# Modulation rows in two or three buffers in turn, narrow loads in their own buffers, and work put off by a tile, in a float32 decoder block

## The chip, the cores and the metric

The kernel runs on one core of one Trainium2 chip. Its metric is the device time of one execution in microseconds (us). The engines of a core work side by side, each on its own queue in program order: TensorE (PE) for matrix products, VectorE (DVE), ScalarE (ACT), GpSimd (POOL), and SyncE (SP), which here issues the transfers.

## The reference

One decoder block on 512 tokens of 1024 features, all in float32. A modulation vector of nine parts shifts, scales and gates three sub-layers: a SwiGLU, a token mixer and a second SwiGLU. A final norm ends it.

```python
mod = silu(c) @ w_ada + b_ada              # 9 x 1024
sh1, sc1, gt1, sh2, sc2, gt2, sh3, sc3, gt3 = split(mod, 9)
h = h + 0.5 * gt1 * swiglu(rmsnorm(h) * (1 + sc1) + sh1)
u = rmsnorm(h) * (1 + sc2) + sh2
p, q, k, v, gate_logits = split(u @ w_in)
y_pool = (trailing means over 2, 4, 8, 16 tokens, minus the token) @ w_pool * pool_scale
q, k = rope(q), rope(k)                    # 12 heads of 64, in 3 groups
y_attn = softmax-weighted sum over groups of dilated window attention(q, k, v)
g_pool, g_attn = split(sigmoid(gate_logits))
h = h + gt2 * ((g_pool * (y_pool @ w_pool_branch) + g_attn * (y_attn @ w_attn_branch)) @ w_out)
h = h + 0.5 * gt3 * swiglu(rmsnorm(h) * (1 + sc3) + sh3)
```

The windows and dilations of the three head groups are (128, 1), (512, 4) and (2048, 16).

## The kernel before, in words

Features lie on the 128 partitions, tokens along the free dimension, so an activation is 8 tiles of 128x512. Each float32 product is made of three matmuls (`mm3`, L353): weight and activation are both split into a high part (rounded) and a low part (the rest), and high x high, high x low and low x high are added in a bank of PSUM.

**Weights.** They come as 128x1024 loads (and some of 128x512) in the order in which they are used. `fetch` (L231) issues the next loads on SyncE's queue as far as buffers are free: three `raw` tiles, and one more during the merge. `split_hi` (L287) makes the high part on ScalarE (L312), `split_lo` (L318) the low part on VectorE (L324), into a ring of 7296 columns. `look` (L333) does this for three or four tiles ahead of the one that TensorE takes next. For products done with fewer multiplications (a Strassen-like scheme on 2x2 blocks: seven products in place of eight) `make` (L250) forms differences of weights on VectorE (L256).

**Modulation rows.** Each of the 72 pieces of `mod` is the sum over a 128x1024 row tile of `w_ada` times `silu(c)`. `ada_fetch` (L370) issues the transfer of a row on SyncE (L374), `ada_do` (L377) makes product and sum on VectorE (L382), and `bg` (L401) is one step of this in the background: it fetches as far as `ada_depth` rows ahead and free buffers allow, makes one product, gives the buffer back and fetches again. The rows 48 to 71 are made in the mixer. From L1271 on they have one buffer, `AR`; after L1343 also `cs`, which held the cosines and sines until then.

**The mixer's attention stage** (`mix`, L1240). Queries and keys of the first head group and its v come first. The loop at L1321 makes the q and k of the groups 1 and 2, in eight tiles of 24 matmuls (`mm_tile`, L1056). Functions hung at a step k of the eight run ahead of that step's matmuls (`hooks`, L1308): at step 5 a piece of attention (scores, maxima and exponentials, a transpose, the product with v), at step 6 the second half of the rotation (`rope_b`, L1050) of the tile before, at step 7 `bg`. Behind a tile's matmuls stands `rope_a` (L1038): ScalarE writes the signed tile to a scratch (L1042), SyncE copies it with the 32-row halves exchanged, in four transfers (L1045), and VectorE multiplies by the cosines (L1047). `rope_b` multiplies the exchanged copy by the sines (L1053) and adds it (L1054). Two tiles with the pooled part follow, whose means GpSimd makes (`pool_diff`, L1199), and then four class tiles with the v of groups 1 and 2: token class c of four, ended by a copy into `v23` (L1375). `v23` is idle between the first rotations, which use it as scratch (L1277), and the second pooling tile.

**The merge** (`merge_out`, L1430). The outputs m = 6, 7, 0, ... 5 are made in pairs. For the last three pairs `gate_duo` (L1393) makes the gate logits in seven products, with ScalarE copying from bank to bank between them (L1396): product 0 goes into bank A, is copied to C, products 2, 4 and 6 are added to A. Then `branch` (L1447), for each of the pair, makes y_pool and y_attn times their branch weights; VectorE multiplies them by the gates and adds them (L1455 to L1457), ScalarE makes the high part (L1458), VectorE the low part (L1459). The high and low parts are read by the output projection only (L1490 to L1505), for whose first two outputs the seven parts other than m = 5 are used first. The gates of the first pair come as plain tiles, whose four sigmoids stand at L1462, ahead of the first branch.

The order of the work on each engine is that of the program text; waits are put in where data or buffers ask for them.

Of the kernel before, what the change touches and what calls it, by code (L numbers as in the profile page):

```python
# [146 lines left out]
class Kernel:  # L147
# [6 lines left out]
    def plan(self):  # L154
# [69 lines left out]
        self.ready = True  # L224
        self.pos, self.held, self.retired, self.half = 0, None, [], None
        self.at, self.start, self.top = {}, {}, 0
        self.buf = {}
# [3 lines left out]
    def fetch(self, n=None):  # L231

        n = len(self.order) - 1 if n is None else min(n, len(self.order) - 1)
        while self.fetched <= self.order[n][1] and self.free:
            i = self.fetched
            name, off, w = self.loads[i]
            src = self.a[name][off:off + P * w].rearrange("(p n) -> p n", p=P)
            self.buf[i] = self.free.pop(0)
            for c in self.pieces(i, w):
                self.nc.sync.dma_start(self.buf[i][:, c], src[:, c])  # L240
            self.fetched += 1
# [76 lines left out]
    def split_lo(self):  # L318
# [9 lines left out]
        for n in [n for n in self.buf if self.last[n] == i]:  # L328
            b = self.buf.pop(n)
            if not any(b is x for x in self.retired):  # L330
                self.free.append(b)

# [44 lines left out]
    def ada_do(self, j, n=1, between=None):  # L377
        t, mod = self.adat.pop(j), self.mod[:, j:j + 1]
        for i in range(n):
# [6 lines left out]
            elif between:  # L386
                between()
        if self.ada_free is not None:
            self.ada_free.append(t)
# [850 lines left out]
    def mix(self):  # L1240
# [10 lines left out]
        with tc.tile_pool(name="rt", bufs=1) as self.rt, tc.tile_pool(name="aw", bufs=2) as self.aw, \  # L1251
# [18 lines left out]
            self.head(1, bk, AF.Exp)  # L1270
            self.ada_free, self.ada_stop, self.ada_depth = [self.AR], 65, 2  # L1271
            self.bg_fetch()
# [14 lines left out]
            for n in range(4):  # L1287
# [11 lines left out]
                for i in ((), (0, 1), (2,), (3,))[n]:  # L1299
                    self.rope_b(*to[i], 1, sw[i])  # L1300
            self.held = None

# [36 lines left out]

            b = self.mm_tile(hooks([], rest + [(6, lambda: by_class(0)), (7, self.bg)]))  # L1340
            self.pool_diff(0, b)

            self.ada_free.append(self.cs)  # L1343
            self.bg_fetch()
            b = self.mm_tile(hooks(g23[0], [(2, lambda: by_class(1)), (3, self.bg), (7, self.bg)]))
# [14 lines left out]
            for c in range(4):  # L1360
                mid = [lambda c=c: by_class(c + 1)] if c in (1, 2) else []
                hk = hooks(g23[c + 1], [(2, self.bg), (7, self.bg)], mid) if c < 3 else \
                    hooks([], [(2, self.at_swap), (2, nxt), (3, nxt), (6, nxt), (7, nxt)])
# [12 lines left out]
            self.held = None  # L1376
            assert self.ada_next == 65 and not self.adat, self.ada_next
            gates = [self.mm_tile(hooks([], [(1, nxt), (3, nxt), (5, self.at_merge)]))]
# [13 lines left out]

    def gate_duo(self, s, c, p5, last):  # L1393

# [10 lines left out]
        for i, (bank, u, start) in enumerate(((A, lambda: blk(lo4, T1), True), (B, lambda: S(0), True),  # L1405
# [3 lines left out]
            if i == 6:  # L1409
                v.tensor_tensor(q(c, 1), q(c, 1), r(p5), op=OP.add)  # L1410
            self.look(4)
            self.product(bank, u(), start, not i)
            if i == 0:
# [3 lines left out]
            elif i == 1:  # L1417
                copy(p5, B)
            elif i == 2:
                copy(q(c, 0), r(A))  # L1420
# [9 lines left out]
    def merge_out(self, ready, last, ma):  # L1430
        nc, tc = self.nc, self.tc
        v = nc.vector
        with tc.tile_pool(name="mg", bufs=1) as mg:
            sc = [mg.tile([P, 2 * T], F32, name=x) for x in ("gs", "gc")]
            p5, raw = mg.tile([P, T], F32, name="p5"), mg.tile([P, D], F32, name="raw")
            self.free.append(raw)
            self.X, self.retired = [self.AR, self.cs], []
            self.ready = True
# [8 lines left out]
            def branch(m):  # L1447
                gp, ga = (x[:, m % 2 * T:(m % 2 + 1) * T] for x in sc)
                self.look()
                w = self.take()  # L1450
                pb, ab = self.nb(), self.nb()
                for b, xh, xl, o in ((pb, self.PH, self.PL, 0), (ab, self.YH, self.YL, 2)):
                    for k in range(2):
                        self.mm3(b, *w[o + k], xh[k], xl[k], k == 0, k == 1)
                v.tensor_tensor(gp, gp, pb, op=OP.mult)  # L1455
                v.tensor_tensor(ga, ga, ab, op=OP.mult)
                v.tensor_tensor(gp, gp, ga, op=OP.add)  # L1457
                nc.scalar.activation(MH[m], gp, AF.Copy)  # L1458
                v.tensor_tensor(ML[m], gp, MH[m], op=OP.subtract)  # L1459

            for i, b in enumerate(ready):
                nc.scalar.activation(sc[i % 2][:, i // 2 * T:(i // 2 + 1) * T], b, AF.Sigmoid)  # L1462
# [26 lines left out]

            kl = [ks(0), ks(1)]  # L1490
            bs = [self.nb(), self.nb()]
# [4 lines left out]
            for m in range(5):  # L1496
# [6 lines left out]
                self.bg()  # L1503
                if m < 2:
                    self.bg()  # L1505
# [7 lines left out]
    def build(self):  # L1513
# [38 lines left out]

        self.ada_free, self.ada_depth = None, 3
        with self.open_ffn():
# [188 lines left out]
```

## Time and profile before

| | |
|---|---|
| median of 3 runs | 1020.76 us (1019.96 to 1021.65) |
| the profiled execution | 1021.9 us |
| its span, first to last instruction | 1020.1 us |
| granted TensorE clock, mean over the span | 0.990 |
| TensorE matmuls busy | 993.1 us (97%) |
| VectorE busy | 788.6 us (77%) |
| ScalarE busy | 475.6 us (47%) |
| GpSimd busy | 30.2 us (3%) |
| read from memory | 135.29 MB |

The attention stage runs from 390.8 to 542.3 us of the span, the merge from there to about 627, the output projection to about 667. A row of a timeline has the start, the duration, the engine, the line, the operation, the tile written and those read, their shapes, the count, and in brackets the idle time ahead of it and what ended it. A row of the waits has who waited, for whom, and the sum in us, the number and the longest. A row of windows has the stretch, its length, then for PE, PEld (weight loads), DVE, ACT and POOL the busy time and the number of instructions, then the granted clock, the share of the transfer engines and GB/s. In the names of tiles `whi` and `wlo` are the high and low parts of weights, `raw`, `AR` and `cs` buffers, `rt` and `tr` scratches of the rotation.

### The profile page before, as it was taken

The page shows a single profiled execution, that of the slowest core. Times are in us where ns is not written, and L with a number is a line of the kernel's source. Part 1 is how long each engine was busy: PE and PEld are TensorE (multiplying, and loading weights), DVE is VectorE, ACT ScalarE, POOL GpSimd, SP SyncE. Part 2 cuts the span into 40 slices and gives each one's busy share as a digit, 9 for nine tenths or more (in the row PEclk, how much of TensorE's full clock was granted, in tenths as well). Part 3 has the DMA queues.
Part 4 walks back from the last instruction along what each step waited for, and adds up shares of the span by engine and source line. Part 5 has one row for each costly group of instructions (what it writes and reads, how often), then busy time and mean ns, then how long its engine had stood idle before and what let it go on. Part 6 is the DMA issues. An engine that isn't in the chain of part 4 may idle for free.

```text
span 1020.1 us, 16353 instructions
## 1 busy us (share of the span) xinstructions
PE 993.1 (97%) x6686; PEld 900.9 (88%) x6686; DVE 788.6 (77%) x1091; ACT 475.6 (47%) x713; POOL 30.2 (3%) x31
## 2 busy tenths in 40 slices
PE   9999999999999999997998999999999999999997
PEld 7888999989899998765778888898899899998997
DVE  7989969898896767767887775877778777776754
ACT  5443643525344554442635453454356345352553
POOL 0000000000000000007200000000000000000002
PEclk9999999999999999998999999999999999999999
DMA  9856445554544425555422225531333325241312
GB/s 341 281 197 220 130 162 182 184 171 165 170 156 135 124 86 150 155 158 182 133 83 76 69 86 185 192 98 62 124 125 126 102 83 166 74 136 53 107 47 83
DMA packets 44876, 141.74 MB, mean 139 GB/s; under 512 B 6273, under 2 KB 9089, under 8 KB 44802
## 3 DMA queue, kind: packets, MB, share of 16 engines
q1 hardware_dynamic: 44226, 140.18, 42.4%
q8 instruction: 52, 0.85, 0.3%
q10 hardware_dynamic: 576, 0.52, 0.2%
q14 instruction: 22, 0.18, 0.1%
HBM read 135.29 MB, written 2.24 MB: 135 GB/s over the span
## 4 chain that ended last, share of the span: by engine, by line
PE 85%; DVE 6%; ACT 3%; DMA 2%; issue 2%; SPq 1%; POOL 0%; POOLq 0%; DVEq 0%; ACTq 0%
PE bank L355 13%; PE bank L356 13%; PE bank L357 13%; PE bank L742 12%; PE bank L743 12%; PE bank L744 12%; PE bank L1669 1%; PE bank L1671 1%; PE bank L1673 1%; DMA rt<-rt 1%; ACT whi L312 1%; DVE AR L382 1%; DVE wlo L324 1%; SPq L1045 1%; DMA rt<-tr 1%
## 5 line engine op out<-in xcount | busy, mean ns | idle before, releaser
L324 DVE TENSOR_TENSOR wlo<-raw,whi 128x1024 fp32r<-128x1024 f32 (+4 forms) x168 | 175.3, 1056 | 54.3 <-ACT whi L312 53.7
L742 PE MATMUL bank<-UH,whi 128*128 128x256 f32 x640 | 177.2, 277 | 0.0
L743 PE MATMUL bank<-UL,whi 128*128 128x256 f32 x640 | 177.2, 277 | 0.0
L744 PE MATMUL bank<-UH,wlo 128*128 128x256 f32 x640 | 177.1, 277 | 0.0
L312 ACT ACTIVATE whi<-raw 128x1024 fp32r<-128x1024 f32 (+4 forms) x168 | 149.9, 910 | 51.7 <-DVE raw L256 47.6
L355 PE MATMUL bank<-HI,whi 128*128 128x512 f32 (+1 forms) x406 | 146.2, 360 | 0.0
L356 PE MATMUL bank<-HK,whi 128*128 128x512 f32 (+1 forms) x406 | 145.9, 359 | 0.0
L357 PE MATMUL bank<-HI,wlo 128*128 128x512 f32 (+1 forms) x406 | 145.8, 359 | 0.0
L324 DVE TENSOR_TENSOR wlo<-X,whi 128x1024 fp32r<-128x1024 f32 (+3 forms) x104 | 111.8, 1083 | 32.4 <-ACT whi L312 32.1
L742 PEld LDWEIGHTS bank<-UH,whi 128*128 128x128 f32 x640 | 120.5, 188 | 0.4
L743 PEld LDWEIGHTS bank<-UL,whi 128*128 128x128 f32 x640 | 120.2, 188 | 0.0
L744 PEld LDWEIGHTS bank<-UH,wlo 128*128 128x128 f32 x640 | 120.1, 188 | 0.0
L742 PE MATMUL bank<-SH,whi 128*128 128x256 f32 x408 | 112.9, 277 | 0.0
L743 PE MATMUL bank<-SL,whi 128*128 128x256 f32 x408 | 112.8, 276 | 0.0
L744 PE MATMUL bank<-SH,wlo 128*128 128x256 f32 x408 | 112.8, 276 | 0.0
L312 ACT ACTIVATE whi<-X 128x1024 fp32r<-128x1024 f32 (+3 forms) x104 | 95.8, 943 | 33.6 <-DVE X L256 32.9
L355 PE MATMUL bank<-UH,whi 128*128 128x512 f32 (+1 forms) x304 | 107.2, 353 | 0.0
L356 PE MATMUL bank<-UL,whi 128*128 128x512 f32 (+1 forms) x304 | 105.8, 348 | 0.1
L357 PE MATMUL bank<-UH,wlo 128*128 128x512 f32 (+1 forms) x304 | 105.6, 347 | 0.0
L357 PEld LDWEIGHTS bank<-HI,wlo 128*128 128x128 f32 x406 | 76.2, 188 | 11.7
L355 PEld LDWEIGHTS bank<-HI,whi 128*128 128x128 f32 x406 | 76.2, 188 | 11.5
L356 PEld LDWEIGHTS bank<-HK,whi 128*128 128x128 f32 x406 | 76.3, 188 | 11.3
(330 smaller groups left out, 1845.0 us busy)
## 6 DMA issues: line engine op xcount, KB each, us to landing
raw<-wmix SPq DMA_DIRECT2D x44, 512.0 KB, 3.8
raw<-wf1i SPq DMA_DIRECT2D x31, 512.0 KB, 4.5
raw<-wf2i SPq DMA_DIRECT2D x30, 512.0 KB, 4.1
AR<-wada SPq DMA_DIRECT2D x25, 512.0 KB, 4.2
ada<-wada SPq DMA_DIRECT2D x23, 512.0 KB, 5.7
cs<-wada SPq DMA_DIRECT2D x16, 512.0 KB, 3.6
X<-wf2i SPq DMA_DIRECT2D x14, 512.0 KB, 3.7
X<-wf1i SPq DMA_DIRECT2D x12, 512.0 KB, 4.4
```

The source lines that it names most:

```text
L312: self.nc.scalar.activation(self.hi[:, y], r[:, x], AF.Copy)
L324: self.nc.vector.tensor_tensor(self.lo[:, y], r[:, x], self.hi[:, y], op=OP.subtract)
L355: M(ps, hi, uh, start=start, stop=False)
L356: M(ps, hi, ul, start=False, stop=False)
L357: M(ps, lo, uh, start=False, stop=stop)
L382: self.nc.vector.scalar_tensor_tensor(t[:, c], t[:, c], 1.0, self.cond[:, c], op0=OP.mult, op1=OP.mult, accum_out=o)
L742: M(o, hi, uh, start=start and p == 0 and k == 0, stop=False, skip_group_check=True)
L743: M(o, hi, ul, start=False, stop=False, skip_group_check=True)
L744: M(o, lo, uh, start=False, stop=k == 3, skip_group_check=True)
L1045: nc.sync.dma_start(w[32 * o:32 * o + 32], t[32 * i:32 * i + 32])
L1669: M(b, hi, self.UH[k], start=k == 0, stop=False)
L1671: M(b, hi, self.UL[k], start=False, stop=False)
```

## The change

1. *Rows.* In the last projection of v of the first group (n = 2) two 4 KB halves of `v23` join `AR` as buffers, and one row product is made there. The loop then has three buffers in turn at depth 2. After the first pooling tile the two halves leave (`ada_gone`: a row in one of them is still used, the buffer is not given back), `cs` joins, and depth is 1. The steps of `bg` move: first pooling tile two in place of one, class tiles one in place of two. Row 64 goes to the output projection, which has three buffers in place of two and eight rows in place of seven.
2. *Narrow loads* of 128x512 (the branch weights) get two buffers of their own in the merge, a piece of `tr` and a new tile.
3. *Work put off.* The four sigmoids, the branches' gate products (`merge`) and the high and low parts (`parts`) go into a list `rest`, of which some are done behind the next `look`: the sigmoids in the first branch, the first branch's products in the second, its parts and the second's products ahead of product 0 of the next `gate_duo`, the second's parts behind product 1; after the last pair between the first splits of the output projection.

```diff
@@ fetch
-        while self.fetched <= self.order[n][1] and self.free:
+        while self.fetched <= self.order[n][1]:
...
+            free = self.small if self.small is not None and w <= T else self.free
+            if not free:
+                break
...
-            self.buf[i] = self.free.pop(0)
+            self.buf[i] = free.pop(0)
@@ split_lo
-                self.free.append(b)
+                (self.small if any(b is x for x in self.smalls) else self.free).append(b)
@@ ada_do
-        if self.ada_free is not None:
+        if self.ada_free is not None and not any(t is x for x in self.ada_gone):
@@ mix
-            self.ada_free, self.ada_stop, self.ada_depth = [self.AR], 65, 2
+            self.ada_free, self.ada_stop, self.ada_depth = [self.AR], 64, 2
...
                 for i in ((), (0, 1), (2,), (3,))[n]:
                     self.rope_b(*to[i], 1, sw[i])
+                if n == 2:
+
+                    mine = [self.v23.rearrange("p n f -> p (n f)")[:, i * D:(i + 1) * D] for i in range(2)]
+                    self.ada_free += mine
+                    self.bg()
...
-            b = self.mm_tile(hooks([], rest + [(6, lambda: by_class(0)), (7, self.bg)]))
+            b = self.mm_tile(hooks([], rest + [(3, self.bg), (6, lambda: by_class(0)), (7, self.bg)]))
             self.pool_diff(0, b)
-            self.ada_free.append(self.cs)
-            self.bg_fetch()
+            self.ada_gone = mine
+            self.ada_free = [x for x in self.ada_free if not any(x is y for y in mine)] + [self.cs]
+            self.ada_depth = 1
...
-                hk = hooks(g23[c + 1], [(2, self.bg), (7, self.bg)], mid) if c < 3 else \
+                hk = hooks(g23[c + 1], [(7, self.bg)], mid) if c < 3 else \
@@ gate_duo
             self.look(4)
+            if not i:
+                rest(2)
             self.product(bank, u(), start, not i)
...
             elif i == 1:
                 copy(p5, B)
+                rest()
@@ merge_out
+            self.small = [self.tr[:, :T], mg.tile([P, T], F32, name="narrow")]
+            self.smalls = list(self.small)
...
                 self.look()
+                if rest:
+                    do()
                 w = self.take()
...
-                v.tensor_tensor(gp, gp, pb, op=OP.mult)
-                v.tensor_tensor(ga, ga, ab, op=OP.mult)
-                v.tensor_tensor(gp, gp, ga, op=OP.add)
-                nc.scalar.activation(MH[m], gp, AF.Copy)
-                v.tensor_tensor(ML[m], gp, MH[m], op=OP.subtract)
-
-            for i, b in enumerate(ready):
-                nc.scalar.activation(sc[i % 2][:, i // 2 * T:(i // 2 + 1) * T], b, AF.Sigmoid)
+                def merge():
+                    v.tensor_tensor(gp, gp, pb, op=OP.mult)
+                    v.tensor_tensor(ga, ga, ab, op=OP.mult)
+                    v.tensor_tensor(gp, gp, ga, op=OP.add)
+
+                def parts():
+                    nc.scalar.activation(MH[m], gp, AF.Copy)
+                    v.tensor_tensor(ML[m], gp, MH[m], op=OP.subtract)
+
+                rest.extend([merge, parts])
+
+            def sigmoids():
+                for i, b in enumerate(ready):
+                    nc.scalar.activation(sc[i % 2][:, i // 2 * T:(i // 2 + 1) * T], b, AF.Sigmoid)
+
+            rest = [sigmoids]
+            do = lambda n=1: [rest.pop(0)() for _ in range(n)]
...
-                    self.gate_duo(*sc, p5, last)
+                    self.gate_duo(*sc, p5, last, do)
...
-            self.ada_free, self.ada_stop = [ma.tile([P, D], F32, name=x) for x in ("k0", "k2")], 72
+            self.ada_free, self.ada_stop, self.ada_depth = [ma.tile([P, D], F32, name=x) for x in ("k0", "k2", "v1")], 72, 2
...
-            kl = [ks(0), ks(1)]
+            kl = [ks(0)]
+            do(2)
+            kl.append(ks(1))
+            do()
...
-                if m < 2:
+                if m < 3:
                     self.bg()
```

More of the change, by code (lines that the diff above doesn't have):

```diff
@@ L225, in plan @@
         self.pos, self.held, self.retired, self.half = 0, None, [], None
+        self.small, self.smalls = None, []
         self.at, self.start, self.top = {}, {}, 0
@@ L1376, in mix @@
             self.held = None
-            assert self.ada_next == 65 and not self.adat, self.ada_next
+            assert self.ada_next == 64 and not self.adat, self.ada_next
             gates = [self.mm_tile(hooks([], [(1, nxt), (3, nxt), (5, self.at_merge)]))]
@@ L1391, in mix, with gate_duo @@
         outer.close()
-    def gate_duo(self, s, c, p5, last):
+    def gate_duo(self, s, c, p5, last, rest):
         nc, v = self.nc, self.nc.vector
@@ L1551, in build @@
         self.scr2 = dram.tile([32, 2 * T], F32, name="scr2")
-        self.ada_free, self.ada_depth = None, 3
+        self.ada_free, self.ada_depth, self.ada_gone = None, 3, []
         with self.open_ffn():
```

## The prediction

> **What bounds the kernel now.** I read the page first, then who waited for whom on TensorE, then stretches of the span with their clock, then the engines' timelines around each wait.
>
> ```profile
> span 1020.1 us, 16353 instructions
> PE 993.1 (97%) x6686; PEld 900.9 (88%) x6686; DVE 788.6 (77%) x1091; ACT 475.6 (47%) x713; POOL 30.2 (3%) x31
> ```
>
> TensorE (PE) is busy for 97% of the span, so a change that leaves the matmuls alone can only win what TensorE waits and what a lowered clock costs it. Its waits of more than 1.1 us in all, by line, are these:
>
> ```profile
> PE bank L742 <- ACT bank L1396: 7.7, 3, 3.5
> PE bank L1091 <- DVE k L1054: 4.5, 1, 4.5
> PE bank L1142 <- DVE v L1375: 3.0, 1, 3.0
> PE bank L1124 <- ACT prob L1112: 2.6, 2, 2.0
> ```
>
> The columns are the sum, the number and the longest. All of them lie in the token mixer: 10.1 us in the attention stage (4.5 + 3.0 + 2.6), 7.7 us in the merge (one wait in each of the three calls of `gate_duo`). The stretches in which the granted clock was halved (column after POOL) lie just behind or in those waits:
>
> ```profile
> 446.40:449.80 3.40, 3.40 (x10) 2.67 (x9) 3.37 (x6) 2.07 (x4) 0.00 (x0) 0.53 0.12 16
> 463.50:470.30 6.80, 4.65 (x13) 3.66 (x14) 5.60 (x5) 0.00 (x0) 6.58 (x5) 0.51 0.20 64
> 487.40:490.80 3.40, 3.40 (x24) 2.74 (x22) 3.26 (x4) 1.20 (x3) 3.17 (x4) 0.52 0.82 237
> 552.20:555.60 3.40, 3.40 (x19) 3.40 (x19) 3.07 (x3) 2.40 (x4) 0.00 (x0) 0.53 0.32 77
> ```
>
> The first number behind the length is PE's busy time; half of it was lost: (3.4 + 4.65 + 3.4) / 2 = 5.7 us in the attention, 1.7 us in the merge. So the prize is 10.1 + 5.7 = 15.8 us in the attention and 7.7 + 1.7 = 9.4 us in the merge, 25.2 us in all.
>
> **The attention stage: rows in three buffers.** One 128x1024 row of the modulation is fetched (L374) and multiplied on VectorE (L382) per tile. With the single buffer `AR` the next fetch waits for the product just made, and it stands in SyncE's queue in front of the four rotation copies (L1045) of the tile. SyncE, then ScalarE, VectorE and TensorE over one tile:
>
> ```profile
> 414.79 0.33 SPq L374 DMA_DIRECT2D AR<-wada  x1
> ...
> 423.30 0.33 SPq L374 DMA_DIRECT2D AR<-wada  x1
> 423.74 2.41 SPq L1045 DMA_DIRECT2D rt<-rt  x4
> ```
>
> ```profile
> 416.98 0.69 ACT L1042 ACTIVATE rt<-bank,cst 128x512 f32<-128x512 f32 x1 [1.41 <-PE bank L357]
> ```
>
> ```profile
> 420.32 0.69 DVE L1053 TENSOR_TENSOR rt<-rt,cs 128x512 f32<-128x512 f32 x1 [3.44 <-DMA rt<-tr]
> ...
> 422.05 1.22 DVE L382 SCALAR_TENSOR_TENSOR AR<-AR,cond 128x1024 f32<-128x1024 f32 x1
> ...
> 425.30 0.41 DVE L1147 COPY o<-bank 128x256 f32<-128x256 f32 x1
> ...
> 428.79 0.69 DVE L1053 TENSOR_TENSOR rt<-rt,cs 128x512 f32<-128x512 f32 x1 [1.30 <-DMA rt<-rt]
> ```
>
> ```profile
> 420.22 1.10 PE L1142 MATMUL bank<-probT,v 128*64 128x128 f32 x16
> 434.69 1.10 PE L1142 MATMUL bank<-probT,v 128*64 128x128 f32 x16
> ```
>
> The copies' source is ready at 416.98 + 0.69 = 417.67; they go out at 423.74, 6.1 us late, because the row's product at 422.05 stands behind the rotation of the tile before, which waited for its own copies (420.32, 3.44 us idle). That is a ring: copies, landing, rotation, row product, fetch, copies. It turns every 423.30 - 414.79 = 8.5 us, while TensorE needs (434.69 - 420.22) / 2 = 7.2 us a tile. TensorE gains on it until it must wait: 2.0 us for the probabilities of the last local block, 4.5 us for the last rotated k.
>
> With three buffers in turn the fetch of row n+2 goes into a buffer whose product was made a tile ago, so nothing holds SyncE. The copies go out when ScalarE is done and land 5.1 us after the first goes out (428.79 - 423.74). The ring is open: rotation of tile i starts 0.7 + 5.1 = 5.8 us after the end of the tile's matmuls. From there VectorE needs 425.30 - 420.32 = 5.0 us to rotation, row product, cosine product and weight split, and in every second tile, from 425.30 until it idles at 428.79 - 1.30 = 427.49, 2.2 us for a copy and the maxima: 2 x 5.0 + 2.2 = 12.2 us a pair against TensorE's 14.5. So VectorE keeps up, and the 2.0 us and the 4.5 us go.
>
> What is late next is VectorE in the two pooling tiles and the first class tile, where GpSimd works (6.58 us in the halved stretch from 463.5, above) and VectorE is slowed:
>
> ```profile
> 463.79 1.81 DVE L1054 TENSOR_TENSOR k<-k,rt 128x512 f32<-128x512 f32 x1
> ...
> 478.81 2.08 DVE L382 SCALAR_TENSOR_TENSOR AR<-AR,cond 128x1024 f32<-128x1024 f32 x1
> ...
> 486.01 0.69 DVE L1375 COPY v<-bank 128x512 f32<-128x512 f32 x1
> ```
>
> ```profile
> 450.21 0.69 ACT L1042 ACTIVATE rt<-bank,cst 128x512 f32<-128x512 f32 x1 [1.74 <-issue]
> ```
>
> ```profile
> DVE AR L382 <- DMA AR<-wada: 2.2, 1, 2.2
> ```
>
> A row product takes 2.08 us there, not 1.22. From the last rotation's end (463.79 + 1.81 = 465.6) to the copy of the first class's values (486.01) are 20.4 us; the change takes out of them one row product of the class tile (2.1 us, the row at 478.81) and VectorE's wait for a row that was fetched only when its buffer was free (2.2 us); 16.1 us stay. One row product is new in the first pooling tile, ahead of the rotation and beside its landing. The last rotation's source, ready at 450.21 + 0.69 = 450.9, comes 3.7 us sooner (the 2.0 us wait and 1.7 us of half clock): with 5.1 us to land and 1.8 us of work the rotation ends at 447.2 + 5.1 + 1.8 = 454.1, in place of 465.6. That gives the copy at 470.2, and TensorE asks for it at 486.84 - 15.8 = 471.0 (its wait of 3.0 us ended 0.8 us after 486.01). Level, then. But GpSimd's stretch now lies beside more of these instructions: three of them at 2.08 - 1.22 = 0.86 us more are 2.6 us, so I book 2.6 - 0.8 = 1.8 us of a new wait here; the ends are 0 and 7 us (the first rival). The scores wanted the last k 4.5 us before 465.6, at 461.1, and 3.7 us sooner after the change, at 457.4: 454.1 is early enough.
>
> The Trainium skill, GPSIMD Engine Reference, section Specifications, says GpSimd shares its SBUF interfaces with VectorE and that they contend when VectorE's instruction has two SBUF inputs. The row product has two, and 2.08 against 1.22 us agrees; it speaks against a change that packs VectorE closer beside GpSimd, and is taken up in the first rival below.
>
> The other moves cost nothing. The first row product now stands in the last projection of v. Cover: VectorE ends the last rotation there at 392.61, and the scores that read it start at 394.33:
>
> ```profile
> 391.92 0.69 DVE L1054 TENSOR_TENSOR k<-k,k 128x512 f32<-128x512 f32 x1
> ```
>
> ```profile
> 394.33 0.72 PE L1091 MATMUL bank<-k,q 64*128 64x128 f32 x8
> ```
>
> 1.22 us fits into 1.72; without that cover it would cost 1.2 us. The fetches into `v23` wait in SyncE's queue for the first copies out of it, with weight fetches behind them; bound 0 to 1 us, taken 0. Row 64 moves to the output projection:
>
> ```profile
> 625.00:667.00 42.00, 42.00 (x243) 36.90 (x241) 32.59 (x50) 16.40 (x23) 0.00 (x0) 1.00 0.53 182
> DVE k L382 <- DMA k<-wada: 1.0, 2, 0.7
> ```
>
> VectorE has 42.0 - 32.6 = 9.4 us of idle there for 1.22 us more, and the third buffer removes the 1.0 us that it waited for rows. Taken 0; without cover 1.2 us.
>
> **The merge: work put off a tile.** In `gate_duo` the third product waits until ScalarE has copied the first out of its bank (L1396). For the second call, ScalarE, VectorE and TensorE:
>
> ```profile
> 576.66 0.64 ACT L1458 ACTIVATE o<-gs 128x512 fp32r<-128x512 f32 x1 [3.21 <-DVE gs L1457]
> ...
> 579.19 1.06 ACT L312 ACTIVATE whi<-raw 128x1024 fp32r<-128x1024 f32 x1 [0.85 <-DVE raw L256]
> 580.15 0.58 ACT L1396 ACTIVATE bank<-bank 128x512 f32<-128x512 f32 x1
> ```
>
> ```profile
> 574.62 0.68 DVE L1455 TENSOR_TENSOR gs<-gs,bank 128x512 f32<-128x512 f32 x1
> ...
> 577.94 1.22 DVE L256 TENSOR_TENSOR raw<-raw,raw 128x1024 f32<-128x1024 f32 x1
> ```
>
> ```profile
> 580.78 0.39 PE L742 MATMUL bank<-v,whi 128*128 128x256 f32 x1 [2.25 <-ACT bank L1396]
> ```
>
> The copy is behind a split (579.19) that waits for a difference on VectorE (577.94), and that is behind the second branch's products and low part, which began at 574.62. Put off, these 577.94 - 574.62 = 3.3 us come after the splits of the first product; the copy moves up by 3.3 us, past the 2.25 us that TensorE waited, with 1.1 us to spare. The same holds for the third call, whose wait was 7.7 - 3.5 - 2.25 = 1.95 us. Nothing else turns late there: low parts and products put off are read only in the output projection, where the last of them has two tiles' matmuls of the other seven parts as cover. So 4.2 us go.
>
> The first call is another matter, because the four sigmoids are put off too:
>
> ```profile
> 535.05 1.28 ACT L1462 ACT_TABLE_LOAD   x1
> ...
> 538.27 1.08 ACT L312 ACTIVATE whi<-AR 128x1024 fp32r<-128x1024 f32 x1
> ...
> 550.95 0.58 ACT L1396 ACTIVATE bank<-bank 128x512 f32<-128x512 f32 x1
> ```
>
> ```profile
> 536.21 1.22 DVE L256 TENSOR_TENSOR AR<-raw,raw 128x1024 f32<-128x1024 f32 x1
> ```
>
> Table and sigmoids took 535.05 to 538.27, 3.2 us; now the split at 538.27 goes first, as soon as its difference is there (536.21 + 1.22 = 537.4), and they end at 537.4 + 1.1 + 3.2 = 541.7. The next split then stands behind them (1.06), and VectorE idles for it; then VectorE's low part (1.2), the first branch's three products (2.0), a difference (1.2), and on ScalarE a split (1.06), the high part (0.64) and the copy (0.58): 541.7 + 1.06 + 1.2 + 2.0 + 1.2 + 1.06 + 0.64 + 0.58 = 549.4. It ended at 551.5, and TensorE wanted it at 551.5 - 3.5 = 548.0. So 1.4 us of the 3.5 stay. The copy behind the third product (line L1396 again) stands behind the split of the seventh product's weights, which comes hardly earlier than before; it holds the fifth product by another 1.2 us. I book 2.6 us; ends 0, and 5.2 (what is lost now, 3.5 + 1.7). Merge: 9.4 - 2.6 = 6.8 us.
>
> Narrow loads in their own buffers let wide weights be fetched a step sooner; no wait of TensorE names a weight fetch, so 0.
>
> **Sum.** Attention 15.8 - 1.8 = 14.0, merge 6.8, rest 0: 20.8 us. The profiled execution took 1021.9 us, 1.8 more than its span; 1021.9 - 20.8 = 1001.1. It lies 1.1 above the median of the runs, 1020.76, so I say 1000.0 us.
>
> The new waits, 1.4 and 1.8 at the longest, are booked at their length only, as the 2.25 and 1.95 us waits of the second and third call were followed by no half clock; but the 2.0 us wait in the attention was. The Trainium skill, TensorE: Matmul & The Clock Gate, section What's actually happening, has the clock halved only after at least one idle window of about 3.4 us: the length of the halved stretches (3.4, 6.8) agrees with such windows, the 2.0 us wait does not. By the rule the sum is as above; by the row one halved stretch more, 1.7 us, and 1001.7 us.
>
> **The rivals.**
> - *VectorE beside GpSimd is the next bound of the attention.* For: the 2.08 us rows, and VectorE busy for 116 of 151 us there (row below). Against: its idle before each rotation (3.44 and 1.30 us above) is slack that the ring forced on it. Half of the attention's gain, 7.0 us, stays away: 1007.0 us. If GpSimd slowed all two-input work for its 24.88 us, VectorE would lose at most 24.88 x (1 - 1.22/2.08) = 10.3 us, in part lost already.
>
> ```profile
> 390.80:542.30 151.50, 140.89 (x754) 110.86 (x753) 116.41 (x215) 65.48 (x133) 24.88 (x20) 0.95 0.46 141
> ```
>
> - *The put-off work only moves the wait*, from the third product to the fifth or to the branches. For: VectorE has no less to do, and the last splits of a call come in the same order. Against: in the second call 3.3 us of it move behind the copy that TensorE waits for. The merge wins nothing: 1020.76 - 14.0 = 1006.8 us.
> - *The buffers don't part*, if a fetch into one half of `v23` is held by the product in the other half. Against: weights of one large tile are written and read piece by piece throughout. The attention keeps its ring and wins only the row product taken from the class tile, 2.1 us, beside the merge's 6.8: 1011.9 us.
> - *Slower: VectorE bounds the mixer already*, its idle being only where it is held by what it feeds itself. Then removed waits come back at the next instruction, and the row product ahead of the scores and the one in the output projection are paid in full: 2.4 us, 1023.2 us. It decides if VectorE's work of a pair of tiles, 12.2 us by the rows, is really over 14.5.
>
> **Chances.** Forecast, 1000.0, 0.62; VectorE beside GpSimd 0.17; wait only moved 0.10; buffers not parted 0.04; slower 0.05; 0.02 for no visible change. A difference under 0.2% (2 us) cannot be told from none. The four first are faster by more than that: 0.93. Range: the lower end is the whole prize, 1020.76 - 25.2 = 995.6, rounded to 995; the upper takes in the two cases at 1007 and a halved stretch or two of 1.7 us on top, 1010. Outside lie the last cases and a little on either side.
>
> **What would show it.** In the attention, SyncE's L1045 right behind L1042, a turn of 7.2 us in place of 8.5; no TensorE wait on L1054 over 1 us, on L1375 under 2; at most one halved stretch. VectorE's L382 at 2 us more often. In the merge, waits on L1396's line gone in the second and third call, 1 to 2 us in the first. Wrong: waits on rotated k or on the class values as long as now, or new TensorE waits on weight splits (L312, L324), or the gain lying outside the mixer.

## The result and the profile after

| | before | after |
|---|---|---|
| median, 4 runs each | 1021.2 us (1019.96 to 1023.55) | 994.74 us (992.92 to 994.86) |
| the profiled execution | 1021.9 us | 994.62 us |
| its span | 1020.1 us | 992.8 us |
| mean granted clock | 0.990 | 1.000 |

The ratio is 0.9734, with a 95% interval of 0.9713 to 0.9755: 2.7% faster. The forecast of 1000.0 us was 5.3 us too high, and the range, which began at 995.0, was missed by 0.3 us.

The busy times from the page of after:

```profile
PE 981.1 (99%) x6686; PEld 893.3 (90%) x6686; DVE 787.2 (79%) x1091; ACT 475.3 (48%) x713; POOL 32.3 (3%) x31
```

The same 6686 matmuls are 12.0 us less busy: most of that is matmuls that ran at half clock before (7.4 us by the prediction's rows) or stood still inside a group that counts as busy (below). TensorE's waits in the mixer, all there are in after from 380 us to 640 us:

```profile
PE bank L747 <- ACT bank L1407: 1.3, 1, 1.3
PE bank L1147 <- DVE v L1386: 0.8, 1, 0.8
PE bank L747 <- ACT gc L1407: 0.6, 1, 0.6
```

These lines answer to L742 on L1396 (7.7 us), L1142 on L1375 (3.0); the waits on the rotated k (4.5) and the probabilities (2.6) are gone. Two stages in after, the attention and the merge:

```profile
390.00:523.80 133.80, 132.95 (x754) 107.12 (x754) 113.91 (x211) 66.37 (x134) 27.00 (x20) 1.00 0.49 162
523.80:600.70 76.90, 74.95 (x580) 71.68 (x580) 62.25 (x76) 43.01 (x61) 0.00 (x0) 1.00 0.34 109
```

The attention took 151.5 us before and now takes 133.8, the merge 85 (542.3 to 627.3) and now 76.9; the clock stands at 1.00 throughout. For the differences below I went by matmuls: both traces have the same 6686 in the same order, so the start of each in one trace can be taken from its start in the other, and what this difference grows by over a stretch is what the stretch won.

| stage | forecast, us | won, us |
|---|---|---|
| attention | 14.0 | 17.7 |
| merge | 6.8 | 8.1 |
| output projection | 0 | 0.0 |
| ahead of the mixer and behind the output projection | 0 | 1.4 |
| sum of span | 20.8 | 27.3 |

Of the 1.4 us, 0.6 lie behind the output projection and show against every kernel below, so they belong to the one profiled execution of before; the rest lies ahead of the mixer's attention, where the kernels are alike and the profiles stand from 0.4 us behind to 1.4 us ahead of that of before.

**The ring is open.** SyncE, ScalarE and VectorE of after, over the pair of tiles behind those that the prediction showed for before:

```profile
425.41 2.41 SPq L1050 DMA_DIRECT2D rt<-tr  x4
...
428.55 0.40 SPq L379 DMA_DIRECT2D v<-wada  x1
431.07 2.41 SPq L1050 DMA_DIRECT2D rt<-rt  x4
...
439.55 2.41 SPq L1050 DMA_DIRECT2D rt<-tr  x4
```

```profile
430.35 0.69 ACT L1047 ACTIVATE rt<-bank,cst 128x512 f32<-128x512 f32 x1 [1.43 <-PE bank L362]
```

```profile
429.36 0.69 DVE L1058 TENSOR_TENSOR rt<-rt,cs 128x512 f32<-128x512 f32 x1 [0.75 <-DMA rt<-tr]
...
435.79 0.42 DVE L1112 CUSTOM_DVE_ANT_0 prob<-bank,masks 128x256 f32<-128x256 f32 x1 [0.62 <-PE bank L1096]
```

The copies go out at 431.07, and ScalarE ended at 430.35 + 0.69 = 431.04: they were 6.1 us late before and aren't late now. Two turns take 439.55 - 425.41 = 14.14 us, 7.1 us a tile. VectorE idles 0.75 us for its copies where it idled 3.44, and at 435.79 it waits for TensorE. What SyncE itself waited for, from 380 to 640 us, in before and in after:

```profile
SPq L374 <- DVE AR L382: 48.3, 10, 7.1
```

```profile
SPq L1050 <- ACT tr L1047: 18.8, 4, 5.3
```

Before, a row's fetch waited for the row product in its buffer, 7.1 us at the longest. After, no fetch waits for a row product in the attention; the copies wait for their own source on ScalarE.

### The profile page after: what moved, and what is told of

It is laid out like the page before. It is cut to its first block, busy times and chain, and to the rows that moved or that the text cites. A ratio compares the mean times of both kernels' runs of the same rounds, so it can differ in the third digit from the quotient of the medians.

```text
span 992.8 us, 16356 instructions
## 1 busy us (share of the span) xinstructions
PE 981.1 (99%) x6686; PEld 893.3 (90%) x6686; DVE 787.2 (79%) x1091; ACT 475.3 (48%) x713; POOL 32.3 (3%) x31
## 3 DMA queue, kind: packets, MB, share of 16 engines
HBM read 135.29 MB, written 2.24 MB: 139 GB/s over the span
## 4 chain that ended last, share of the span: by engine, by line
PE 87%; DVE 6%; ACT 2%; issue 2%; DMA 2%; SPq 0%; POOL 0%; POOLq 0%; DVEq 0%; ACTq 0%
PE bank L360 14%; PE bank L361 14%; PE bank L362 14%; PE bank L747 13%; PE bank L748 12%; PE bank L749 12%; PE bank L1702 1%; PE bank L1704 1%; PE bank L1706 1%; DVE wlo L329 1%; DMA H<-xT 1%; DVE ut L467 1%; PE bank L1147 1%; DVE UL L493 1%; PE bank L1096 0%
## 5 line engine op out<-in xcount | busy, mean ns | idle before, releaser
L329 DVE TENSOR_TENSOR wlo<-raw,whi 128x1024 fp32r<-128x1024 f32 (+4 forms) x162 | 172.8, 1079 | 49.7 <-ACT whi L317 49.4
L317 ACT ACTIVATE whi<-raw 128x1024 fp32r<-128x1024 f32 (+4 forms) x162 | 146.3, 921 | 57.6 <-DVE raw L261 54.1
```

What stands on the lines that cost most here:

```text
L317: self.nc.scalar.activation(self.hi[:, y], r[:, x], AF.Copy)
L329: self.nc.vector.tensor_tensor(self.lo[:, y], r[:, x], self.hi[:, y], op=OP.subtract)
```

## The experiments

Every kernel was timed beside the kernel before on the same chip. "Won" is by matmuls against the profiled execution of before; in stages that a kernel leaves alone it came out between -2.1 and +0.4 us, and so a microsecond or two of it means nothing.

**The rows alone**, put into the kernel before (point 1 of the change; nothing put off, no narrow buffers).

```diff
+                    mine = [self.v23.rearrange("p n f -> p (n f)")[:, i * D:(i + 1) * D] for i in range(2)]
+                    self.ada_free += mine
+                    self.bg()
...
+            self.ada_gone = mine
+            self.ada_depth = 1
```

> The kernel before with the rows' part alone: three buffers, the moved steps, row 64 in the output projection. If the attention's gain is all the rows' own (17.7 us between the start of the q and k loop and the first gate product, by the two profiles), the time is 1021.2 - 17.7 = 1003.5 us, and the three waits on L1396 of the kernel before, 7.7 us, stay as they are. If part of that stage's gain needs the work put off, the time lies above 1005 us.

Measured: 1004.87 us, ratio 0.9837 (0.9809 to 0.9864) to 1021.51. The attention won 18.7 us. The waits left in the mixer:

```profile
PE bank L742 <- ACT bank L1402: 7.7, 3, 3.5
```

The merge's waits are untouched, and it ran 2.0 us longer, for the clock was halved there in 10.2 us of it and not in 3.4. So the rows are worth the whole gain of the attention, without the rest.

**The change without the rows' part**: work put off and narrow buffers only.

```diff
-                    self.ada_free += mine
-                    self.bg()
...
-            self.ada_gone = mine
+            self.ada_free.append(self.cs)
+            self.bg_fetch()
```

> The changed kernel with the rows' part undone. If the two parts add up, the merge's 8.1 us go and nothing else: 1021.2 - 8.1 = 1013.1 us, with the attention's waits (4.5, 3.0, 2.6 us) and its three halved stretches as before. If the put-off only works because the stage starts earlier, or the wait only moves, less than 4 us go: over 1017 us.

Measured: 1014.47 us, ratio 0.9932 (0.9905 to 0.9958) to 1021.51. The merge won 8.5 us, the attention lost 1.8. TensorE's waits in the attention:

```profile
PE bank L1096 <- DVE k L1059: 5.0, 1, 5.0
PE bank L1129 <- ACT prob L1117: 3.9, 3, 1.8
PE bank L1147 <- DVE v L1380: 3.0, 1, 3.0
```

These are the three waits of before, 1.8 us longer in sum; the merge's, not shown, are the two of after (1.3 and 0.8 us here, 1.3 and 0.6 there). The two parts hold separate stages; in medians they make 16.6 + 7.0 = 23.6 of the 26.5 us; of the 2.9 us between, 2.0 are what the rows alone lost in the merge.

**The moved steps alone**: row products at their new places, one buffer.

```diff
+                if n == 2:
+                    self.bg()
...
-            b = self.mm_tile(hooks([], rest + [(6, lambda: by_class(0)), (7, self.bg)]))
+            b = self.mm_tile(hooks([], rest + [(3, self.bg), (6, lambda: by_class(0)), (7, self.bg)]))
...
-                hk = hooks(g23[c + 1], [(2, self.bg), (7, self.bg)], mid) if c < 3 else \
+                hk = hooks(g23[c + 1], [(7, self.bg)], mid) if c < 3 else \
```

> The kernel before with the row products moved as in the change (one earlier, one taken from each class tile, row 64 to the output projection) but with the one buffer AR, joined by cs after the first pooling tile. If the ring through SyncE's queue was the bound, it keeps its turn of 8.5 us and the wait on the last rotated k; only the product taken from the class tile, 2.1 us, and part of the wait on the class values go: 1017 to 1020 us. If the moved steps and not the buffers made the gain, about 1003.5 us.

Measured: 1020.39 us, ratio 0.9984 (0.9964 to 1.0004) to 1021.51. The waits on the class values and on k:

```profile
PE bank L1091 <- DVE k L1054: 7.8, 1, 7.8
...
PE bank L1142 <- DVE v L1377: 1.2, 1, 1.2
```

The wait for the class values, whose tile has a product less, fell from 3.0 to 1.2 us, and the wait for k, whose last rotation has a product more ahead of it, grew from 4.5 to 7.8. With the ring closed the moves give nothing.

**The buffers alone**: every step at its old place, row 64 in the class tiles.

```diff
+                    self.ada_free += mine
+                    self.bg_fetch()
```

> The kernel before with the two halves of v23 as further row buffers in the loop, but every row product at its old step (none in the v projection, one in the first pooling tile, two in the class tiles; row 64 stays). If the ring was the bound, the waits on the probabilities (2.0 us) and on the last rotated k (4.5 us) and their halved stretches go, and the wait on the class values (3.0 us) stays in part, as the class tile has two products again: 1005 to 1010 us. If the moved steps made the gain, 1018 us or more.

Measured: 1003.53 us, ratio 0.9819 (0.9804 to 0.9834) to 1021.6. The attention won 16.6 us. The only wait left in the attention:

```profile
PE bank L1142 <- DVE v L1380: 2.0, 1, 2.0
```

I had expected a smaller gain. The buffers make nearly all of the attention's gain; the moved steps take out the 2.0 us for the class values.

**Two buffers, still two rows ahead.** If any second buffer will do, this is as fast as the change; if what counts is that SyncE waits for the product just made, it closes the ring again, since the fetch of row n+2 needs the buffer of row n.

```diff
-                    mine = [self.v23.rearrange("p n f -> p (n f)")[:, i * D:(i + 1) * D] for i in range(2)]
+                    mine = [self.v23.rearrange("p n f -> p (n f)")[:, i * D:(i + 1) * D] for i in range(1)]
```

> The changed kernel with one half of v23 in place of two, so two row buffers in the loop, and the fetch still two rows ahead. Every fetch then goes into the buffer whose product was made just before it, as with one buffer, only a row later. If what counts is that the fetch in front of the copies must wait for the product just made, the ring is back, with its turn of 8.5 us, and nearly the whole gain of the attention stage is lost (16.6 us between the run with the moved steps alone and the changed kernel): 1008 to 1012 us. If a second buffer is enough in itself, 994 to 997 us.

Measured: 1007.88 us, ratio 0.9877 (0.9854 to 0.9901) to 1020.77. The attention won 6.5 us in place of 17.7. SyncE:

```profile
423.66 0.33 SPq L379 DMA_DIRECT2D AR<-wada  x1
424.09 2.41 SPq L1050 DMA_DIRECT2D rt<-rt  x4
...
432.34 0.33 SPq L379 DMA_DIRECT2D v<-wada  x1
432.77 2.41 SPq L1050 DMA_DIRECT2D rt<-tr  x4
```

The fetch is again ahead of the copies, one tile takes 432.34 - 423.66 = 8.7 us, and TensorE waits 4.1 us for the rotated k.

**Two buffers, one row ahead.** The same, with depth 1.

```diff
-            self.ada_free, self.ada_stop, self.ada_depth = [self.AR], 64, 2
+            self.ada_free, self.ada_stop, self.ada_depth = [self.AR], 64, 1
```

> The same two buffers, but the fetch one row ahead: it goes into the other buffer, whose product was made a tile before. If the waiting fetch in front of the copies is the cause, the ring is open with two buffers: at most 3 us above the changed kernel (in the pooling tiles, where two products stand four matmul steps apart, a row that takes 4 us to land comes late): 994 to 998 us. If three buffers are needed because rows must be fetched two ahead, 1008 us or more.

Measured: 994.59 us, ratio 0.9746 (0.9725 to 0.9768) to 1020.77; the change itself had 994.65 on that chip. SyncE:

```profile
428.15 0.40 SPq L379 DMA_DIRECT2D v<-wada  x1
430.67 2.41 SPq L1050 DMA_DIRECT2D rt<-rt  x4
```

With the same memory as the run before, 13.3 us apart: what counts is that the fetch's buffer has been free for a tile when it is issued. The third buffer adds nothing here.

**The rows on another queue.** One buffer, but the fetches of rows 48 to 64 issued by GpSimd, so that they can't stand ahead of the copies.

```diff
+            q = self.nc.gpsimd if 48 <= j < 65 else self.nc.sync
-            self.nc.sync.dma_start(t[:, c], self.a["wada"][j * P:(j + 1) * P, c])
+            q.dma_start(t[:, c], self.a["wada"][j * P:(j + 1) * P, c])
```

> The kernel before, one buffer, old steps; only the fetches of the rows 48 to 64 are issued from GpSimd's queue, so that the rotation copies no longer stand behind them on SyncE. If the copies' place behind the waiting fetch was the cost, the ring opens here too, until the pooling tiles, where GpSimd is busy with the means and its queue holds the fetches: the 2.0 and 4.5 us waits go, 1007 to 1013 us. If it was the single buffer itself (a row landing too late), the waits stay: 1019 to 1022 us.

Measured: 1025.88 us, ratio 1.0029 (1.0008 to 1.0051) to 1021.6. The expectation failed. TensorE's waits, and the longest of VectorE for a row:

```profile
PE bank L1143 <- DVE v L1376: 8.7, 2, 8.1
...
PE bank L1092 <- DVE k L1055: 0.6, 1, 0.6
```

```profile
DVE AR L383 <- DMA AR<-wada: 14.5, 3, 10.8
```

The wait on k went from 4.5 to 0.6 us, as the ring wants it. But now the fetches and the means stand in one queue. The means, whose source was ready at 452.6 us, began at 459.4, behind a fetch that had waited 5.4 us for its buffer; and a later fetch went out only behind the last of the means, at 488.60 us, so that VectorE waited 10.8 us for that row and TensorE 8.1 us for class values behind it. The run moves the blocking to another queue and doesn't weigh the ring by itself.

**The sigmoids back in their old place**, everything else as changed.

```diff
-            rest = [sigmoids]
+            rest = []
+            sigmoids()
```

> The changed kernel with the four sigmoids back at their place ahead of the first branch's splits, all else put off. If putting the sigmoids off is what left the first call its 1.3 and 0.6 us (VectorE idle for 3.05 us until the split behind them), both go: 994.7 - 1.9 = 992.8 us. If those two waits come from the branch's products and differences on VectorE, it stays at 994.7 us; if the sigmoids in front delay the first splits more than they free, 995.5 to 997 us.

Measured: 992.12 us, ratio 0.9713 (0.9687 to 0.9738) to 1021.51. The merge won 10.8 us, not 8.1, and no wait of TensorE is left in it. First the change, ScalarE and VectorE in the first call of `gate_duo`, then this kernel:

```profile
518.98 1.06 ACT L317 ACTIVATE whi<-AR 128x1024 fp32r<-128x1024 f32 x1 [2.43 <-DVE AR L261]
520.06 1.28 ACT L1487 ACT_TABLE_LOAD   x1
...
523.28 1.08 ACT L317 ACTIVATE whi<-cs 128x1024 fp32r<-128x1024 f32 x1
...
530.29 0.58 ACT L1407 ACTIVATE bank<-bank 128x512 f32<-128x512 f32 x1
```

```profile
524.39 1.23 DVE L329 TENSOR_TENSOR wlo<-cs,whi 128x1024 fp32r<-128x1024 f32 x1 [3.05 <-ACT whi L317]
```

```profile
516.73 1.28 ACT L1487 ACT_TABLE_LOAD   x1
...
520.89 1.08 ACT L317 ACTIVATE whi<-cs 128x1024 fp32r<-128x1024 f32 x1
...
528.09 0.58 ACT L1407 ACTIVATE bank<-bank 128x512 f32<-128x512 f32 x1
```

In the change the table and the sigmoids stand between the first two splits, and VectorE idles 3.05 us for the second. Early, they fill time in which ScalarE waits for a difference anyway (the 2.43 us at 518.98), and the copy ends 2.2 us sooner. So putting off the sigmoids costs the change 10.8 - 8.1 = 2.7 us; putting off products and parts is what pays. (The narrow buffers are in both kernels; alone they give nothing, as the next run shows, and the put-off work without them was not run.)

**Narrow buffers alone**, in the kernel before.

```diff
+            free = self.small if self.small is not None and w <= T else self.free
...
-            self.buf[i] = self.free.pop(0)
+            self.buf[i] = free.pop(0)
```

> The kernel before with the two own buffers for the narrow loads alone. No wait of TensorE names a weight fetch, so nothing changes: 1020.2 to 1022.2 us. If the wide weights' earlier fetch had a part in the merge's gain, 1 to 3 us less.

Measured: 1021.3 us, ratio 1.0000 (0.9984 to 1.0017) to 1021.6: nothing.

**The change without GpSimd's means.** They are left out of the pooled branch, and ScalarE copies the projected tile in their place. It ran once, so the trace says more than the time.

```diff
-        while w < 2 * w0:
+        while w < 0:
...
-        for half, w in ((0, w0), (1, 2 * w0)):
+        nc.scalar.activation(d, p[:, 16:], AF.Copy)
+        for half, w in ():
```

> The changed kernel without GpSimd's trailing means and differences (ScalarE copies the projected tile in their place, so the pooled branch is left out of the computation). If GpSimd's sharing with VectorE makes the one wait left in the attention (0.8 us on the class values), VectorE's two-input instructions there take 1.2 us and not 2.1, the wait goes, and the time is 993 to 994 us. If VectorE is late there by its own work, the wait stays and so does the time, 994.7 us.

Measured: 992.99 us. VectorE's end of the last rotation, a row product behind it and the copy of the class values in after, then row product and copy here:

```profile
450.74 1.08 DVE L1059 TENSOR_TENSOR k<-k,rt 128x512 f32<-128x512 f32 x1
...
454.88 2.08 DVE L387 SCALAR_TENSOR_TENSOR v<-v,cond 128x1024 f32<-128x1024 f32 x1
...
467.93 1.21 DVE L387 SCALAR_TENSOR_TENSOR cs<-cs,cond 128x1024 f32<-128x1024 f32 x1
...
469.08 0.68 DVE L1386 COPY v<-bank 128x512 f32<-128x512 f32 x1
```

```profile
454.16 1.22 DVE L387 SCALAR_TENSOR_TENSOR v<-v,cond 128x1024 f32<-128x1024 f32 x1
...
465.85 0.69 DVE L1387 COPY v<-bank 128x512 f32<-128x512 f32 x1
```

The class values come 3.2 us sooner and TensorE's wait for them is gone. So GpSimd's means made that wait, as booked, but it is 0.8 us and not 1.8, and it hangs on how the instructions of the two engines fall: the rows alone, with the same attention and the means, had none.

**A version that combines**: sigmoids early, and the first class tile's row product (row 63) moved to the output projection, to take away the last wait of the attention. The change itself ran again beside it.

```diff
-            self.ada_free, self.ada_stop, self.ada_depth = [self.AR], 64, 2
+            self.ada_free, self.ada_stop, self.ada_depth = [self.AR], 63, 2
...
-                hk = hooks(g23[c + 1], [(7, self.bg)], mid) if c < 3 else \
+                hk = hooks(g23[c + 1], [(7, self.bg)] if c else [], mid) if c < 3 else \
...
-                if m < 3:
+                if m < 4:
```

> The changed kernel with the four sigmoids at their old place and the row product of the first class tile moved to the output projection (row 63, so 15 rows in the attention stage and nine there). The sigmoids' place is worth 2.6 us by the earlier run, the row product takes VectorE 1.2 us ahead of the copy of the class values, which TensorE waited 0.8 to 0.9 us for: 991.2 us, and no wait of TensorE over 0.3 us in the mixer. If that wait has another cause it stays, at 992.1 us; if the output projection is full, 992.5 to 994 us.

> The changed kernel once more, beside the next one on the same chip: 994.7 us.

Measured: 991.5 us (991.19 to 992.35), ratio 0.9716 (0.9698 to 0.9734) to 1020.77; the change 994.65 us (993.06 to 995.78), ratio 0.9744 (0.9724 to 0.9764). The four runs of one lie below the four of the other, 3.1 us apart in the medians. The attention won 18.7 and the merge 10.8 us, the output projection gave back 0.5. No wait of TensorE over 0.3 us is left in the mixer.

## Where the prediction was right, and where it failed

**The step that failed is the first: "So the prize is 10.1 + 5.7 = 15.8 us in the attention and 7.7 + 1.7 = 9.4 us in the merge, 25.2 us in all."** The mechanism held, this size didn't. In the attention 17.7 us were won while 0.8 us of a new wait stayed, so TensorE had lost 18.6 us there, 2.8 more than the list of waits and the halved clock show; in the merge 8.1 + 1.3 + 0.6 = 10.0 us, 0.6 more. The list shows the long wait ahead of a group of matmuls. Within a group the matmuls can wait one after another for their pieces, each time about 0.2 us, too short to be listed. The transposes of the probabilities, in before and in after:

```profile
444.56 1.92 PE L1124 MATMUL bank<-cst,prob 128*128 128x128 f32 x8 [2.04 <-ACT prob L1112]
...
453.49 1.09 PE L1142 MATMUL bank<-probT,v 128*64 128x128 f32 x16
```

```profile
441.27 1.04 PE L1129 MATMUL bank<-cst,prob 128*128 128x128 f32 x8
```

The group before took 1.92 us at a full clock, and 0.9 of it was waiting, put down as busy; the one at 474.69 did the same. These two are 1.8 of the 2.8 us. The rest, by the starts of the matmuls: 0.3 us in the transposes at 427.90, 0.4 us in the first class tile's matmuls from 478.4, and 0.15 us each right behind the two listed waits for probabilities. In the merge too a wait cost more than its listed length, as the matmuls right behind it start late: against after, 2.53 us for the one of 2.25 and 2.24 for the one of 1.97. The loss could have been read from the trace of before alone, by the pace of like work. The product with v follows at 434.69 and 453.49, 18.8 us, where the pair of tiles ahead of it took 14.5; after, the pairs take these times:

```profile
419.46 1.09 PE L1147 MATMUL bank<-probT,v 128*64 128x128 f32 x16
...
433.60 1.09 PE L1147 MATMUL bank<-probT,v 128*64 128x128 f32 x16
...
447.71 1.09 PE L1147 MATMUL bank<-probT,v 128*64 128x128 f32 x16
```

14.14 and 14.11 us. The pair had lost 4.7 us, of which the prediction's rows gave 2.0 + 1.7 = 3.7. Since the range ended at "the whole prize", the same slip set its lower end.

**The second error has the same sign: new waits booked too large.** 1.8 us for the class values are 0.8. Here the sum had two slips. It let TensorE ask 15.8 us sooner than 486.84, but 1.7 of these lie in the halved stretch from 487.4, behind that point: 472.7, not 471.0. And it took 0.8 us off as slack, which is the time from the copy's start to the matmuls: with the booked 2.6 us the copy starts at 470.2 + 2.6 = 472.8 and the matmuls at 473.6. So by the prediction's own rows the wait was 0.9 us. Measured, the copy started at 469.08 and TensorE asked at 469.05, both 3.7 us sooner: the losses that the list left out lie mostly ahead of this point. In the merge 1.4 + 1.2 = 2.6 us were booked for the put-off sigmoids; 1.3 + 0.6 are there, 0.7 less. Together the two errors are 2.8 + 1.0 + 0.6 + 0.7 = 5.1 us. With the 1.4 us outside the stages they are the 6.5 us from the prediction's 1001.1 to the profiled 994.62; by the medians it was 5.3.

Point by point:

- *The ring.* Right, and shown: it opens with the buffers alone (won 16.6 us), stays closed with the moved steps alone, and closes again with two buffers at depth 2.
- *VectorE keeps up*, 12.2 us a pair. Right: busy 12.44 us in the pair of 14.14 us of after, and it waits for TensorE.

```profile
419.46:433.60 14.14, 14.14 (x81) 11.31 (x81) 12.44 (x24) 6.42 (x15) 0.00 (x0) 1.00 0.58 186
```

- *Moved steps cost nothing.* Right within 0.1 us in the output projection. They are not worthless: with the ring open they take 2.0 us off the class values (buffers alone against rows alone).
- *Second and third call of the merge*: 4.2 us of waits go. Right, no wait is left there. The copy of the second call now follows its split and high part at once:

```profile
553.26 1.07 ACT L317 ACTIVATE whi<-raw 128x1024 fp32r<-128x1024 f32 x1 [3.31 <-DVE raw L261]
...
554.74 0.58 ACT L1407 ACTIVATE bank<-bank 128x512 f32<-128x512 f32 x1
```

- *First call*: the put-off sigmoids keep 1.4 us of the wait at the third product. Right (1.3), and shown by putting them back.
- *Narrow loads*: 0. Right in the kernel before; beside the put-off work not tested.
- *"At most one halved stretch"*: none.
- *The rivals.* VectorE beside GpSimd is there, at 0 to 0.9 us and not at 7.0. The wait moved only in the first call. The buffers part. VectorE doesn't bound the mixer: the slower case has no trace of itself.

The Trainium skill, GPSIMD Engine Reference, section Specifications, has VectorE's two-input instructions contend with GpSimd for shared SBUF interfaces; the row product of 2.08 us beside the means and 1.22 without them agrees. Not every one beside them is slow: in after the one that began at 454.88, while an addition of GpSimd ran (453.95 to 455.87), took 2.08 us, and the one at 467.93, with GpSimd's next addition beginning at 468.07, took 1.21.

## What to carry to other kernels

When a transfer waits for a buffer, look at what stands behind it on the issuing queue: a ring through that queue slows everything in it, and a second buffer opens it only if the fetch goes into the buffer that has been free for a step (two buffers one ahead: 994.6 us, two ahead: 1007.9). Measure what an engine loses by the pace of like work in two places, not by adding up the list of its waits, which leaves out those inside a group. Put off what is read late, but leave work where it fills a wait that is there anyway.

## What was not expected of the hardware

The halved clock comes in slots. In before the halved stretches that the prediction shows start at 446.4, 463.5, 487.4 and 552.2 us; the distances to the first are 17.1, 41.0 and 105.8 us, 5.0, 12.0 and 31.0 times 3.413, and each is one or two times 3.41 long. The same holds within every run here that has more than one (in one a stretch is three times 3.41 long). What halves the next slot is how long TensorE stood in one. Two pairs of neighbouring slots in the kernel with the moved steps alone, whose waits in the merge are 2.25 and 1.98 us:

```profile
602.33:605.74 3.41, 1.44 (x14) 1.24 (x12) 3.41 (x4) 2.47 (x4) 0.00 (x0) 1.00 0.00 0
605.75:609.15 3.40, 3.40 (x16) 3.40 (x17) 3.40 (x4) 2.41 (x3) 0.00 (x0) 0.50 0.33 77
575.03:578.43 3.40, 1.54 (x14) 1.34 (x12) 3.07 (x5) 2.54 (x5) 0.00 (x0) 1.00 0.00 0
578.45:581.85 3.40, 3.03 (x26) 3.03 (x27) 3.40 (x4) 2.84 (x4) 0.00 (x0) 1.00 0.23 77
```

In the first slot TensorE stood 3.41 - 1.44 = 1.97 us, and the next ran at 0.50; in the third it stood 3.40 - 1.54 = 1.86 us, as the longer wait ended in the slot behind, and the next ran at 1.00. In the mixers of all runs here no slot at full clock with up to 1.5 us of standing was followed by a halved one, and every one with over 1.9 was; three of 1.6 to 1.9 us that were hold the stretched transposes, whose 0.9 us count as busy, and the other three of that size were not. That answers the prediction's question about the 2.0 us wait that halved the clock while 2.25 us didn't. The Trainium skill, TensorE: Matmul & The Clock Gate, section What's actually happening, has free-running windows of 3413 ns: the runs agree. It asks for an idle window, and here a window idle for 1.9 of its 3.4 us was enough. A slot already halved needs less to keep the next one halved: in the same mixers 0.97 us of standing or more did, and behind 0.27 us or less the next ran at full clock. So in these runs, at full clock, waits that add up to less than 1.9 us in a slot cost no more than their standing, and one of 2 to 3 us may cost 1.7 us more, by where it falls; removing other waits moves it against the slots, as in the rows alone, whose merge ran 2.0 us longer with the waits of before.
